# Ten more plain weight splits on VectorE, the first two weights loaded in halves, and the last quarter's first Down outputs behind the last seventh product

## The chip, the cores and the metric

One core of one Trainium2 chip runs the whole kernel. The metric is the device time of one execution in microseconds (us), the median over several runs. Engines are named as the profile names them: PE (TensorE, the matrix unit), DVE (VectorE), ACT (ScalarE), POOL (GpSimd), SP (SyncE, which issues most loads).

## The reference, cut to what matters

A decoder of two layers over 512 tokens of width 1024, all in float32. Each layer is a half-step feed-forward block, a token mixer of three head groups, a second half-step feed-forward block and a norm:

```python
for l in range(2):
    h = x + 0.5 * swiglu(rms_norm(x, ffn1_norm[l]), ffn1_w1[l], ffn1_w3[l], ffn1_w2[l])
    n = rms_norm(h, mix_norm[l])
    u_conv, q, k, v, q_mem = jnp.split(n @ w_in[l], splits, axis=-1)
    y_conv = conv_module(u_conv, ...)       # GLU, causal depthwise conv of 31 taps over 384 channels, LayerNorm, swish
    y_swa = sliding_window_attention(q, k, v, swa_sinks[l])   # after QK-norm and rotary
    y_mem = memory_attention(qm, mk, mv)
    h = h + jnp.concatenate([y_conv, y_swa, y_mem], axis=-1) @ w_out[l]
    h = h + 0.5 * swiglu(rms_norm(h, ffn2_norm[l]), ffn2_w1[l], ffn2_w3[l], ffn2_w2[l])
    x = rms_norm(h, final_norm[l])

def swiglu(x, w1, w3, w2):                   # w1, w3: 1024 x 2816, w2: 2816 x 1024
    return (jax.nn.silu(x @ w1) * (x @ w3)) @ w2
```

## The kernel before, in words

The residual stream `h` stays on chip as 128 partitions x 8 blocks x 512 tokens. Weights come from HBM in units of 128 x 1024 (512 KB) or less into a `raw` buffer, of which there are three.

**Split products.** PE multiplies rounded operands, so every operand is kept as a high part and a low part, and one product term is three matmuls (`mm3`): high x high (L161), low activation x high weight (L162), high activation x low weight (L163). A plain projection (`project`) has 8 such terms, 24 matmuls of 128 x 512. What makes the parts of a weight is `weights(src, cols, on)`:
- with `on` = V it calls `split`: ACT copies `raw` to `whi` (L135), VectorE subtracts to get `wlo` (L136);
- with `on` = G it calls `split_by_dma`: ACT copies `raw` to `whi` (L140) and its negative to `wlo` (L141), and then POOL issues a DMA that loads the same weights from HBM a second time and adds them onto `wlo` (L142).

There are four `whi`/`wlo` pairs, so a pair comes free when the product before the last three has been multiplied. The same line L136 also makes the low parts of activations (`xlo`, `ml`, `glo`).

**A feed-forward block.** 22 hidden blocks of 128. The first four (`PLAIN`) are computed plainly, eight projections (`up`): w1 and w3 of each. Then nine pairs of hidden blocks follow, each by the seven products of a Strassen scheme (`up_pair`) on half-width operands: matmuls of 128 x 256 into the PSUM tiles `po` and `pt`, with the high parts of operands made by ACT and the low parts by VectorE. The Down projection (w2) runs in four `QUARTERS` of 6, 6, 6 and 4 hidden blocks. `begin(d)` loads a Down weight for output block d and multiplies all but its last two hidden blocks; the loop after it adds the last two, then VectorE adds the result into `h`. In the first three quarters the next pair of hidden blocks is computed first and one output is begun at a time; in the last quarter (`ahead` is 0) the first three outputs are begun ahead of the last seventh product's results.

**Start.** `h`, the first two weights and small tables are loaded by SP. For each of the eight blocks of `h`, ACT and VectorE make `xhi` (L145) and `xlo` (L146), and POOL squares the block (L215); VectorE adds the squares into `st` (L229). PE sums `st` over the partitions (`cf`, L186) between the second and the third projection, VectorE makes the mean (`ms`, L192), POOL takes the power -1/2 (`rsq`, L178), PE spreads it over the tokens (`pt`, L199), ACT copies it (`R`, L204), and VectorE makes the normed activations for the seven products (`n`, L256). The rotary tables (L459 to L492 on VectorE, `sn` L496 and `cs` L497 on ACT) are made in the same stretch.

**Mixer.** The convolution's 384 channels are three chunks `c` of 128; each needs two projections (GLU value and gate). They and the query projections run while VectorE does the 93 taps of the depthwise convolution, of which the 90 accumulating ones are L744. `head_scale` and its ACT squares (`hsq`, L512) stand between, with VectorE rows L514, L515 and L519.

**Order.** Every engine works through a fixed queue. A scheduler sets the order of independent instructions by its own estimate of times when the program is built; `queued()` overrides it for a block of code: the block's PE instructions are put on PE's queue right behind the last PE instruction traced before.

Of the kernel before, what the change touches and what calls it, by code (L numbers as in the profile page):

```python
# [10 lines left out]
F32 = mybir.dt.float32  # L11
# [7 lines left out]
P = 128  # L19
D = 1024  # L20
# [19 lines left out]
UNIT = 1024  # L40
# [19 lines left out]
def trunk(ctx: ExitStack, tc: tile.TileContext, xT, memT, pos, w1a, w3a, w2a, w1b, w3b, w2b,  # L60
          wconv, wqk, wvm, wmem, wout, gains, small, rows, consts, out):
    nc = tc.nc
    V, G, A, T = nc.vector, nc.gpsimd, nc.scalar, nc.tensor
# [3 lines left out]
    wst = ctx.enter_context(tc.tile_pool(name="wst", bufs=4))  # L67
# [8 lines left out]
    def queued():  # L76

        return tc.issue_after(tail[0].ins)
# [18 lines left out]
    def raw_tile(src, cols):  # L97
        raw = wst.tile([P, UNIT], F32, tag="raw", name="raw", bufs=3)
        nc.sync.dma_start(raw[:, 0:cols], src)
        return raw  # L100
# [3 lines left out]
    gn = const.tile([P, L, 5, KD], F32, name="gn")  # L104
    nc.sync.dma_start(gn, gains)
    first = []
    for k in range(KD):
        nc.sync.dma_start(h[:, k, :], xT[:, k, :])
        if k in (0, 3):
            first.append(raw_tile((w1a, w3a)[k // 3][0, 0], D))  # L110
    cst = const.tile([P, P + 256 + 32], F32, name="cst")
    nc.sync.dma_start(cst, consts)
    ident = cst[:, 0:P]
# [20 lines left out]
    def split(hi, lo, x, on):  # L134
        A.activation(hi, x, AF.Copy)  # L135
        on.tensor_tensor(out=lo, in0=x, in1=hi.bitcast(F32), op=ALU.subtract)  # L136
# [11 lines left out]
    def pair():  # L148
        return (wst.tile([P, UNIT], F32R, tag="whi", name="whi"), wst.tile([P, UNIT], F32R, tag="wlo", name="wlo"))

    def weights(src, cols, on):
        raw = first.pop(0) if first else raw_tile(src, cols)
        hi, lo = pair()
        if on is G:
            split_by_dma(hi[:, 0:cols], lo[:, 0:cols], raw[:, 0:cols], src)
        else:
            split(hi[:, 0:cols], lo[:, 0:cols], raw[:, 0:cols], on)
        return hi, lo
# [12 lines left out]
    def project(ps, w, x):  # L171

        for k in range(KD):
            mm3(ps, at(w, ALL, blk(k)), at(x, ALL, k, ALL), k == 0, k == KD - 1)
# [208 lines left out]
    def ffn(l, w13, w2, x, sums, factors, last, at_product, aside=None):  # L383
# [2 lines left out]

        def up(f, i):
            ps = bank([P, S], "po" if 2 * f + i in (3, 4) else "mm")
            project(ps, weights(w13[i][l, f], 1024, V if f == 0 else G), x)
            return ps  # L390

        def gate(pp, R, u, g, hi, lo):
# [29 lines left out]
        for q, (f0, nf) in enumerate(QUARTERS):  # L422
            ahead = 2 if q + 1 < len(QUARTERS) else 0
            for f in range(f0, f0 + nf + ahead, 2):
                if f not in g:
                    g[f], g[f + 1] = up_pair(l, w13, f, M)
            begun = []

            def begin(d):

                w = weights(w2[l, d, :, f0 * P : (f0 + nf) * P], nf * P, V)
                ps = bank([P, S], "mm")
                for j in range(nf - 2):
                    mm3(ps, at(w, ALL, blk(j)), g[f0 + j], j == 0, False)
                begun.append((ps, w))

            for d in range(KD):
                while len(begun) < (d + 1 if ahead or d else 3):
                    begin(len(begun))
                ps, w = begun[d]  # L440
                for j in range(nf - 2, nf):
                    mm3(ps, at(w, ALL, blk(j)), g[f0 + j], False, j == nf - 1)
                V.scalar_tensor_tensor(out=h[:, d, :], in0=ps, scalar=0.5, in1=h[:, d, :], op0=ALU.mult, op1=ALU.add)  # L443
                if not ahead:
                    last(d)
            if aside and not q:
                aside()
# [139 lines left out]
    def mixer(l, x, st, last):  # L587
# [31 lines left out]
        def conv_in(c):  # L619
            nonlocal R  # L620
            pp = []
            for i in range(2):
                with queued() if 2 * c + i < 3 else nullcontext():
                    ps = mm()
                    project(ps, weights(wconv[l, c, i], 1024, G if c == 2 else V), x)
                    pp.append(ps)
                if c == 0:
                    with queued():
                        if i == 0:
                            V.tensor_copy(rc, rms_cols(st, D))  # L630
                        else:
                            R = kept(spread(rc), "R")
            u, s = ypad[:, c, PAD:], ring("cv")
            V.tensor_tensor(out=u, in0=pp[0], in1=R, op=ALU.mult)
            V.tensor_tensor(out=s, in0=pp[1], in1=R, op=ALU.mult)
            A.activation(s, s, AF.Sigmoid)
            V.tensor_tensor(out=u, in0=u, in1=s, op=ALU.mult)
# [128 lines left out]
        for step in ORDER.split():  # L766
            f = {"c": conv_in, "q": queries, "v": values, "w": window, "r": recall, "t": taps, "s": swish}[step[0]]
# [4 lines left out]
        for d in range(KD):  # L772
            w = weights(wout[l, d, :, CCH:], 640, V)
            ps = bank([P, S], ("mm", "mm", "mm", "cf", "po", "po", "pt", "pt")[d])
# [3 lines left out]
        for d in range(KD):  # L778
            w = weights(wout[l, d, :, 0:CCH], CCH, V)
# [3 lines left out]
            last(d)  # L783


    st = Stat("st", on=G)
    nxt = Next(gn[:, 0, N_FFN1], (st, None))
    for d in range(KD):
        nxt(d)

    def stages(st, gain):
# [5 lines left out]
    for l in range(L):  # L797
        x, new = nxt.x, Stat("st")
# [110 lines left out]
```

## Time and profile before

| | |
|---|---|
| time, median of 3 runs | 1847.12 us (1841.6, 1847.12, 1849.46) |
| profiled execution | 1840.85 us, its span 1839.1 us |
| granted clock, mean | 0.988 |
| PE busy | 1777.9 us (97% of the span) |
| DVE busy | 1297.8 us (71%) |
| ACT busy | 895.5 us (49%) |
| POOL busy | 188.3 us (10%) |
| DMA | 248.87 MB, of which 56.63 MB in the queue of POOL's transfers |

The profile is of one execution. A row of the timeline gives an instruction's start, its duration, its engine, line and tiles, and in brackets how long the engine sat idle ahead of it and what ended that wait. Matmuls are pipelined: a row of 0.39 us for 128 x 512 is followed by the next one 0.23 us later at full clock and 0.43 us later at half clock, so the distance of starts is what a matmul costs. VectorE's rows overlap by some 0.07 us in the same way.

### The profile page before, as it was taken

Reading aid. Unit: us, or ns where it says so; the run is one execution under the profiler, and the core shown is the slowest. Engines: PE = TensorE matmul, PEld = TensorE weight load, DVE = VectorE, ACT = ScalarE, POOL = GpSimd, SP = SyncE. Lnnn points to the kernel's source line nnn. Section 1 sums busy time; section 2 is a strip of 40 time slices with the busy share of each in tenths; the row PEclk is TensorE's granted clock in tenths of the full one; section 3 lists DMA queues with packets and bytes.
Section 4 is the critical chain, followed back from the end, with each engine's and each line's share of the span. In section 5 each row is a group of like instructions: output and inputs, shape, how many; then the busy total and the mean of one; then the engine's idle time right before and its main releaser. Section 6 shows DMA issues by size and latency. Waiting matters only on the chain.

```text
span 1839.1 us, 28085 instructions
## 1 busy us (share of the span) xinstructions
PE 1777.9 (97%) x10892; PEld 1581.9 (86%) x10892; DVE 1297.8 (71%) x1978; ACT 895.5 (49%) x1459; POOL 188.3 (10%) x194
## 2 busy tenths in 40 slices
PE   6999999998899999999999999999989999999997
PEld 5989999877677989898888898988776889898986
DVE  7967666579956866666678586666789577675755
ACT  5556444354656535453565463535456455353532
POOL 4001000005101000000010010000240010000000
PEclk8999999999999999999999999999999999999998
DMA  9565645263038556565465565643530576474622
GB/s 278 125 172 159 177 130 155 63 159 101 15 77 200 118 141 167 143 169 141 133 154 139 160 170 141 170 118 92 117 105 1 144 162 158 134 181 122 171 78 75
DMA packets 92437, 248.87 MB, mean 135 GB/s; under 512 B 9488, under 2 KB 11792, under 8 KB 92304
## 3 DMA queue, kind: packets, MB, share of 16 engines
q1 hardware_dynamic: 76752, 190.45, 34.0%
q0 software_dynamic: 15552, 56.63, 17.3%
q8 instruction: 85, 1.39, 0.3%
q14 instruction: 48, 0.39, 0.1%
HBM read 244.95 MB, written 2.10 MB: 134 GB/s over the span
## 4 chain that ended last, share of the span: by engine, by line
PE 76%; DVE 10%; issue 7%; DMA 4%; ACT 2%; POOL 1%; SPq 0%; POOLq 0%; DVEq 0%; ACTq 0%
PE mm L162 11%; PE mm L163 10%; PE mm L161 10%; PE po L163 8%; PE po L161 8%; PE po L162 8%; PE pt L161 5%; PE pt L162 5%; PE pt L163 5%; DVE there L744 3%; DVE wlo L136 1%; DMA wlo<-in_w1a 1%; DVE xlo L146 1%; DMA wlo<-in_wconv 1%; DVE st L229 1%
## 5 line engine op out<-in xcount | busy, mean ns | idle before, releaser
L135 ACT ACTIVATE whi<-raw 128x1024 fp32r<-128x1024 f32 (+4 forms) x372 | 342.3, 924 | 513.3 <-PE mm L162 263.9
L136 DVE TENSOR_TENSOR wlo<-raw,whi 128x1024 fp32r<-128x1024 f32 (+4 forms) x372 | 392.0, 1056 | 123.8 <-ACT whi L135 122.5
L162 PE MATMUL mm<-glo,whi 128*128 128x512 f32 x752 | 293.9, 391 | 1.0 <-DVE glo L136 1.0
L161 PE MATMUL mm<-ghi,whi 128*128 128x512 f32 x752 | 289.8, 391 | 5.2 <-ACT ghi L379 4.5
L163 PE MATMUL mm<-ghi,wlo 128*128 128x512 f32 x752 | 292.8, 389 | 0.0
L163 PE MATMUL po<-mh,wlo 128*128 128x256 f32 x864 | 244.6, 283 | 1.4 <-DVE wlo L136 1.4
L161 PE MATMUL po<-mh,whi 128*128 128x256 f32 x864 | 244.8, 283 | 0.0
L162 PE MATMUL po<-ml,whi 128*128 128x256 f32 x864 | 244.6, 283 | 0.0
L161 PE MATMUL pt<-xhi,whi 128*128 128x256 f32 x864 | 243.4, 283 | 1.0 <-DVE g L347 0.7
L163 PE MATMUL pt<-xhi,wlo 128*128 128x256 f32 x864 | 243.9, 283 | 0.0
L162 PE MATMUL pt<-xlo,whi 128*128 128x256 f32 x864 | 243.8, 283 | 0.0
L443 DVE SCALAR_TENSOR_TENSOR h<-mm,h 128x512 f32<-128x512 f32 x128 | 87.7, 688 | 134.5 <-PE mm L163 134.5
L161 PEld LDWEIGHTS mm<-ghi,whi 128*128 128x128 f32 x752 | 140.9, 188 | 35.9 <-ACT ghi L379 6.2
L161 PEld LDWEIGHTS pt<-xhi,whi 128*128 128x128 f32 x864 | 165.1, 192 | 3.0 <-DVE g L347 1.1
L163 PEld LDWEIGHTS po<-mh,wlo 128*128 128x128 f32 x864 | 165.8, 192 | 1.6 <-DVE wlo L136 1.6
L162 PEld LDWEIGHTS mm<-glo,whi 128*128 128x128 f32 x752 | 141.4, 188 | 30.0 <-DVE glo L136 1.9
L162 PEld LDWEIGHTS pt<-xlo,whi 128*128 128x128 f32 x864 | 165.7, 192 | 1.1
L161 PEld LDWEIGHTS po<-mh,whi 128*128 128x128 f32 x864 | 165.8, 192 | 0.9 <-ACT part L366 0.2
L163 PEld LDWEIGHTS mm<-ghi,wlo 128*128 128x128 f32 x752 | 141.2, 188 | 29.2
L162 PEld LDWEIGHTS po<-ml,whi 128*128 128x128 f32 x864 | 165.8, 192 | 0.6
L163 PEld LDWEIGHTS pt<-xhi,wlo 128*128 128x128 f32 x864 | 165.5, 192 | 0.0
L744 DVE SCALAR_TENSOR_TENSOR there<-ypad,par,there 128x512 f32<-128x512 f32 x180 | 133.7, 759 | 0.7
(272 smaller groups left out, 3306.4 us busy)
## 6 DMA issues: line engine op xcount, KB each, us to landing
raw<-in_w2a SPq DMA_DIRECT2D x48, 384.0 KB, 3.7
raw<-in_w2b SPq DMA_DIRECT2D x48, 384.0 KB, 4.0
raw<-in_w1a SPq DMA_DIRECT2D x26, 512.0 KB, 3.7
raw<-in_w3a SPq DMA_DIRECT2D x26, 512.0 KB, 4.3
raw<-in_w1b SPq DMA_DIRECT2D x26, 512.0 KB, 3.8
raw<-in_w3b SPq DMA_DIRECT2D x26, 512.0 KB, 3.7
wsum<-in_w1a SPq DMA_DIRECT2D x18, 512.0 KB, 4.5
wsum<-in_w3a SPq DMA_DIRECT2D x18, 512.0 KB, 4.5
```

The source lines that it names most:

```text
L135: A.activation(hi, x, AF.Copy)
L136: on.tensor_tensor(out=lo, in0=x, in1=hi.bitcast(F32), op=ALU.subtract)
L146: V.scalar_tensor_tensor(out=lo, in0=x, scalar=col, in1=hi.bitcast(F32), op0=ALU.mult, op1=ALU.subtract)
L161: T.matmul(ps, a[0], b[0], start=first, stop=False, **more)
L162: T.matmul(ps, a[0], b[1], start=False, stop=False, **more)
L163: tail[0] = T.matmul(ps, a[1], b[0], start=False, stop=last, **more)
L229: V.tensor_tensor(out=self.sums[0], in0=self.sums[0], in1=sq, op=ALU.add)
L443: V.scalar_tensor_tensor(out=h[:, d, :], in0=ps, scalar=0.5, in1=h[:, d, :], op0=ALU.mult, op1=ALU.add)
L744: V.scalar_tensor_tensor(out=cv[:, c, :], in0=ypad[:, c, j : j + S], scalar=conv_w[:, c, j : j + 1], in1=cv[:, c, :], op0=ALU.mult, op1=AL ...
```

## The change

Four edits:
1. The first two weights (w1 and w3 of hidden block 0) are loaded as halves of 128 x 512, the first of them ahead of `h`, and their parts are made half by half, on VectorE as before.
2. In layer 0's first feed-forward block the six other plain weights are split on VectorE (`split`) and not by DMA; so are the two weights of convolution chunk 2, in both layers. In total ten second loads of 512 KB, with their DMA issues on POOL and their negative copies on ACT, go, and ten subtracts of 128 x 1024 come.
3. Of the eight initial squares of `h`, two (blocks 2 and 5) are taken by ACT, six by POOL.
4. In the last quarter of each Down projection the first three `begin(d)` stand in `queued()`.

```diff
     first = []
+    for w in (w1a, w3a):
+        first.append(wst.tile([P, UNIT], F32, tag="raw", name="raw", bufs=3))
+    halves = [slice(i * 512, i * 512 + 512) for i in range(2)]
+    nc.sync.dma_start(first[0][:, halves[0]], w1a[0, 0, :, halves[0]])
     for k in range(KD):
         nc.sync.dma_start(h[:, k, :], xT[:, k, :])
-        if k in (0, 3):
-            first.append(raw_tile((w1a, w3a)[k // 3][0, 0], D))
+        if k == 1:
+            nc.sync.dma_start(first[0][:, halves[1]], w1a[0, 0, :, halves[1]])
+        if k in (4, 5):
+            nc.sync.dma_start(first[1][:, halves[k - 4]], w3a[0, 0, :, halves[k - 4]])
...
     def weights(src, cols, on):
-        raw = first.pop(0) if first else raw_tile(src, cols)
         hi, lo = pair()
+        if first:
+            raw = first.pop(0)
+            for c in halves:
+                split(hi[:, c], lo[:, c], raw[:, c], V)
+            return hi, lo
+        raw = raw_tile(src, cols)
...
-            project(ps, weights(w13[i][l, f], 1024, V if f == 0 else G), x)
+            project(ps, weights(w13[i][l, f], 1024, V if f == 0 or l == 0 and w13[0] is w1a else G), x)
...
                 while len(begun) < (d + 1 if ahead or d else 3):
-                    begin(len(begun))
+                    with nullcontext() if ahead or d else queued():
+                        begin(len(begun))
...
-                    project(ps, weights(wconv[l, c, i], 1024, G if c == 2 else V), x)
+                    project(ps, weights(wconv[l, c, i], 1024, V), x)
...
-    st = Stat("st", on=G)
+    st = Stat("st")
     nxt = Next(gn[:, 0, N_FFN1], (st, None))
     for d in range(KD):
+        st.on = G if d % 3 < 2 else None
         nxt(d)
```

The line numbers of the kernel after are higher: L161 to L163 become L172 to L174, L136 becomes L142, L146 becomes L152, L229 becomes L240, L459 to L497 become L471 to L509, L744 becomes L756.

VectorE's queue at the start, before, from the last squares to the first rows of the rotary tables (`st` is the sum of squares, `ms` the mean, `ypad` a buffer that the tables use as scratch):

```order
L146 SCALAR_TENSOR_TENSOR xlo<-h,gn,xhi 128x512 x3
L229 TENSOR_TENSOR st<-st,sq 128x512
L131 TENSOR_SCALAR nsink<-rw 128x12
L537 TENSOR_TENSOR gmem<-rw 128x64
L229 TENSOR_TENSOR st<-st,sq 128x512 x3
L192 TENSOR_SCALAR ms_230<-cf 128x4
L466 CAST pf<-posi 128x4
L467 TENSOR_TENSOR ypad<-cst,pf 128x128
L459 TENSOR_SCALAR ypad<-ypad 128x128
```

The same place after:

```order
L152 SCALAR_TENSOR_TENSOR xlo<-h,gn,xhi 128x512 x2
L137 TENSOR_SCALAR nsink<-rw 128x12
L549 TENSOR_TENSOR gmem<-rw 128x64
L240 TENSOR_TENSOR st<-st,sq 128x512 x2
L142 TENSOR_TENSOR wlo<-raw,whi 128x1024
L240 TENSOR_TENSOR st<-st,sq 128x512
L142 TENSOR_TENSOR wlo<-raw,whi 128x1024
L203 TENSOR_SCALAR ms_236<-cf 128x4
L478 CAST pf<-posi 128x4
L479 TENSOR_TENSOR ypad<-cst,pf 128x128
```

The subtract of the third plain weight now stands ahead of the last sum of squares, that of the fourth ahead of `ms`. Two more stand among the first rows of the tables, the last two among the gates of the plain blocks; 28 rows of the tables and the six products `sg`, `cg` with them, which all stood ahead of `n` (L256), now stand behind it.

PE's queue at the end of the last seven-product pair of a block, before (`pt` is the last seventh product, `mm` with `ghi`, `glo` are Down outputs; the row with x3 is the first that needs the gated result of this pair):

```order
L162 MATMUL pt<-xlo,whi 128x256
L163 MATMUL pt<-xhi,wlo 128x256
L161 MATMUL mm<-ghi,whi 128x512
L162 MATMUL mm<-glo,whi 128x512
L163 MATMUL mm<-ghi,wlo 128x512
L161 MATMUL mm<-ghi,whi 128x512
L162 MATMUL mm<-glo,whi 128x512
L163 MATMUL mm<-ghi,wlo 128x512
L161 MATMUL mm<-ghi,whi 128x512 x3
```

The same place after:

```order
L174 MATMUL pt<-xhi,wlo 128x256
L172 MATMUL mm<-ghi,whi 128x512
L173 MATMUL mm<-glo,whi 128x512
L174 MATMUL mm<-ghi,wlo 128x512
L172 MATMUL mm<-ghi,whi 128x512
L173 MATMUL mm<-glo,whi 128x512
L174 MATMUL mm<-ghi,wlo 128x512
L172 MATMUL mm<-ghi,whi 128x512
L173 MATMUL mm<-glo,whi 128x512
L174 MATMUL mm<-ghi,wlo 128x512
L172 MATMUL mm<-ghi,whi 128x512
L173 MATMUL mm<-glo,whi 128x512
```

Of the 18 matmuls of the three begun outputs, six stood behind the last seventh product before; the other twelve stood between the last two products and ahead of them. All 18 stand behind it now, and the last two products follow each other at once.

VectorE's queue in layer 0's mixer, before, where the two projections of convolution chunk 2 run (`hv` is a row of `head_scale`, `cg`, `sg` are rotary factors):

```order
L744 SCALAR_TENSOR_TENSOR there<-ypad,par,there 128x512
L515 TENSOR_SCALAR hv_4113<-hs_4112 128x8
L744 SCALAR_TENSOR_TENSOR there<-ypad,par,there 128x512
L533 TENSOR_TENSOR cg<-cs,rw 128x4x64
L659 TENSOR_TENSOR gg<-gg 128x512
L533 TENSOR_TENSOR cg<-cs,rw 128x4x64
L744 SCALAR_TENSOR_TENSOR there<-ypad,par,there 128x512 x2
L136 TENSOR_TENSOR wlo<-raw,whi 128x640
```

After:

```order
L756 SCALAR_TENSOR_TENSOR there<-ypad,par,there 128x512
L527 TENSOR_SCALAR hv_4113<-hs_4112 128x8
L142 TENSOR_TENSOR wlo<-raw,whi 128x1024
L756 SCALAR_TENSOR_TENSOR there<-ypad,par,there 128x512
L142 TENSOR_TENSOR wlo<-raw,whi 128x1024
L545 TENSOR_TENSOR cg<-cs,rw 128x4x64
L671 TENSOR_TENSOR gg<-gg 128x512
L142 TENSOR_TENSOR wlo<-raw,whi 128x640
```

The two new subtracts of 128 x 1024 stand right behind `hv`, one tap apart.

## Prediction

> **What bounds the kernel now.** I read the busy times first, then PE's waits, then the timeline at each wait. The page's first line, and PE's waits, each with their total, their number and the longest:
>
> ```profile
> PE 1777.9 (97%) x10892; PEld 1581.9 (86%) x10892; DVE 1297.8 (71%) x1978; ACT 895.5 (49%) x1459; POOL 188.3 (10%) x194
> ```
>
> ```profile
> PE mm L161 <- ACT whi L135: 7.2, 1, 7.2
> PE mm L163 <- DMA wlo<-in_wconv: 5.0, 2, 2.7
> PE mm L161 <- ACT ghi L379: 4.5, 4, 1.1
> PE po L163 <- DMA wlo<-in_w1a: 2.1, 1, 2.1
> PE mm L163 <- DMA wlo<-in_w1a: 2.0, 1, 2.0
> ```
>
> PE is the bound, so only time taken out of PE's own row counts. The change touches all five of these, 20.8 us in sum, of which 7.2 is mostly the wait for the first bytes; two more places stand in the rows below. Beside the waits stands the clock. The windows below have PE busy time, granted clock, DMA share and GB/s in slices at the start (first two) and in layer 0's mixer:
>
> ```profile
> 23.89:27.31 3.42, 2.60 (x10) 0.67 0.71 111
> 30.72:34.13 3.41, 3.41 (x9) 0.50 1.04 259
> 450.56:453.97 3.41, 0.72 (x2) 0.67 0.99 224
> 453.97:457.39 3.42, 3.13 (x7) 0.50 1.02 278
> ```
>
> After a wait of about 2 us PE runs at half clock until it has been fully busy for some 3.4 us: a wait is paid a second time.
>
> The Trainium skill, "TensorE: Matmul & The Clock Gate", section "The two states you'll see" of the clock gate, drops the clock after an idle window of about 3.4 us. The trace does not agree in the letter: PE had worked 0.72 us in the slice in which the clock fell. By the page's rule no wait left over in the start below would cost clock, and the sum would be 1.7 us better; I go by the rows.
>
> **The start (edits 1 to 3).** Rows of PE, then of ACT and VectorE:
>
> ```profile
> 24.64 1.53 PE L186 MATMUL cf<-onesq,st 128*128 128x1 f32 x8 [1.79 <-DVE st L229]
> 26.04 0.77 PE L161 MATMUL mm<-xhi,whi 128*128 128x512 f32 x1
> 29.29 0.80 PE L163 MATMUL mm<-xhi,wlo 128*128 128x512 f32 x1 [2.05 <-DMA wlo<-in_w1a]
> 37.20 1.05 PE L199 MATMUL pt<-cst,rsq 128*128 128x128 f32 x8
> 46.32 0.50 PE L163 MATMUL po<-xhi,wlo 128*128 128x512 f32 x1 [2.14 <-DMA wlo<-in_w1a]
> 36.49 0.31 ACT L496 ACTIVATE sn<-ypad 128x128 f32<-128x128 f32 x1 [10.12 <-DVE ypad L492]
> 39.92 0.57 ACT L204 ACTIVATE R<-pt 128x512 f32<-128x512 f32 x1
> 40.53 2.08 DVE L256 SCALAR_TENSOR_TENSOR n<-h,gn,R 128x512 f32<-128x512 f32 x3 [0.67 <-ACT R L204]
> ```
>
> Up to 24.64 VectorE sets the pace, and its groups between 0 and 130 us cost:
>
> ```profile
> L136 DVE TENSOR_TENSOR wlo<-raw,whi 128x1024 fp32r<-128x1024 f32 x12 | 15.3, 1278 | 1.2 <-ACT whi L135 0.9
> L146 DVE SCALAR_TENSOR_TENSOR xlo<-h,gn,xhi 128x512 fp32r<-128x512 f32 x8 | 9.0, 1149 | 2.7 <-ACT xhi L145 2.7
> L380 DVE SCALAR_TENSOR_TENSOR glo<-g,ghi 128x512 fp32r<-128x512 f32 x4 | 2.6, 682 | 0.0
> ```
>
> The `xlo` rows take 1149 ns, the like rows of `glo`, made when POOL is quiet, 682 ns. One added subtract (1.14 us from start to start: 1.22 where POOL is quiet, as the like 128x1024 row of L376 further down has it, less the rows' overlap) goes ahead of the last sum of squares; against it stand two fewer POOL squares beside VectorE and first bytes that come 256 KB sooner. SP issues two more loads for the halves, POOL ten fewer accumulating ones, so POOL's powers and `wsum` loads wait for less than before; I cost both at nothing. I take the column sums at 23.5 us, 1.1 earlier (between 22.0, if every `xlo` came down to 682 ns, 8 x 0.47 = 3.7 less the 1.14, and 24.6, if nothing is won).
>
> The Trainium skill, "SBUF — State Buffer", section "Who interferes with whom", says that VectorE with two SBUF inputs and GpSimd share a port pair and lock each other out. It speaks against subtracts put on VectorE beside POOL's squares; the trace agrees (1149 against 682 ns). By it the one subtract that stands ahead of the last sum could cost 1149/682 times its 1.14, 0.8 us more, within my bounds.
>
> From there: column sums and the bank take 1.4 us (24.64 to 26.04, the third product's first start), the product's 24 matmuls at 0.227 us take 5.45, and one window at half clock costs 1.7, since PE still idles ahead of the sums. Before, this product lasted from 26.04 to 37.20, 11.2 us, with the 2.05 us wait for the accumulating DMA in it. So PE spreads at 32.0 and not at 37.20, 5.2 earlier. `R` came 2.7 us behind that only because ACT stood in its queue behind `sn`, 10.12 us on VectorE's tables; the tables are behind now, and `R` is ready 1.05 + 0.57 and some 0.2 us after the spread begins, t_R = 33.8 against 40.5 (32.1 with no half clock, 35.5 with two windows of it). The later 2.14 us wait goes too, so PE, left alone, would be 5.2 + 2.1 = 7.3 us ahead at the first seven-product pair, which follows the eighth product.
>
> What is late next is VectorE, which took over two more subtracts behind `R` and the tables that moved there:
>
> ```profile
> 46.00:92.00 46.00, 45.68 (x297) 41.99 (x298) 43.37 (x60) 23.70 (x33) 2.58 (x3) 1.00 0.51 125
> 92.00:138.00 46.00, 46.00 (x268) 40.83 (x267) 30.71 (x46) 23.38 (x39) 1.73 (x2) 1.00 0.61 172
> 40.53:105.66 65.13, 59.15 (x82) 1.00 0.57 145
> 26.22:40.53 14.31, 12.37 (x56) 0.68 1.03 232
> 104.70 0.96 DVE L136 TENSOR_TENSOR wlo<-raw,whi 128x768 fp32r<-128x768 f32 x1 [1.69 <-ACT whi L135]
> 105.63 0.40 PE L163 MATMUL mm<-ghi,wlo 128*128 128x512 f32 x1
> ```
>
> The first two rows have the busy times of PE, PEld, DVE, ACT, POOL; VectorE is 94% busy from 46 to 92 us. The next two are VectorE alone. The first of them runs from `R` to the use of the first Down weight's low part at 105.63: 59.15 busy, 0.96 of it the second Down subtract, so 58.2. To this come 2 x 1.14 = 2.3 for subtracts, and the 28 table rows and six factors, which stood in the stretch from 26.22 on: 34 of its 56 instructions, so 7.5 of its 12.37 us, where each row waits for the one before it; set among other rows they start some 0.07 us before their predecessor's end, which leaves 5.1. 65.6 of work and about 3 of waits for PE and ACT that stay, 68.6: the low part is there at 33.8 + 68.6 = 102.4, 3.2 us ahead of before. So VectorE lets the pair keep 3.2 and not 7.3. I take 3 us for the start; 0.7 if the table rows cost their 7.5, 1.5 with two windows of half clock, 7.3 if VectorE's waits shrink and PE stays the bound. Behind 105 us VectorE has room (30.71 of 46 us is its busy time from 92 to 138), so nothing further is lost.
>
> **The convolution's third chunk (edit 2), per layer.**
>
> ```profile
> 450.83 0.50 PE L161 MATMUL mm<-xhi,whi 128*128 128x512 f32 x1 [1.59 <-ACT hsq L512]
> 454.26 0.79 PE L163 MATMUL mm<-xhi,wlo 128*128 128x512 f32 x1 [2.70 <-DMA wlo<-in_wconv]
> 449.53 0.16 DVE L515 TENSOR_SCALAR hv<-hs 128x8 f32<-128x8 f32 x1
> 461.60 0.69 DVE L634 TENSOR_TENSOR ypad<-mm,R 128x512 f32<-128x512 f32 x1 [3.54 <-PE mm L163]
> 467.53 0.69 DVE L635 TENSOR_TENSOR aux<-mm,R 128x512 f32<-128x512 f32 x1 [1.41 <-PE mm L163]
> 470.00:522.00 52.00, 46.77 (x283) 34.41 (x282) 49.48 (x140) 34.67 (x123) 4.94 (x4) 0.93 0.02 7
> 1365.57 0.69 DVE L634 TENSOR_TENSOR ypad<-mm,R 128x512 f32<-128x512 f32 x1 [2.97 <-PE mm L163]
> 1371.73 0.69 DVE L635 TENSOR_TENSOR aux<-cf,R 128x512 f32<-128x512 f32 x1 [0.55 <-PE cf L163]
> ```
>
> PE loses 1.6 + 2.7 and then about 2.3 to half clock. But the mixer is VectorE's: 49.48 of 52 us busy from 470 on, and PE's loss counts only as VectorE's idle time, 3.54 + 1.41 = 4.95 us here, waiting for these projections. The new subtracts stand right behind `hv` (449.53), a tap apart, so both low parts are there by 452.6, some 1.7 us before the old one; with the half clock gone too the product ends at 461.6 - 2.7 - 2.3 = 456.6, ahead of VectorE's need even with 2 x 1.14 = 2.28 us more of rows. Net 4.95 - 2.28 = 2.7 in layer 0. In layer 1 the idle time is 2.97 + 0.55 = 3.5: net 1.2. Sum 3.9. Below: idle time unchanged and the subtracts added, -2.28 per layer, -4.6. Above: the subtracts fall into idle time that stays elsewhere, +8.5.
>
> **The last Down quarters (edit 4), four times.**
>
> ```profile
> 362.62 0.28 PE L163 MATMUL pt<-xhi,wlo 128*128 128x256 f32 x1
> 362.94 0.42 DVE L347 TENSOR_TENSOR g<-pt,part 128x256 f32<-128x256 f32 x1 [3.08 <-PE pt L163]
> 363.47 1.23 DVE L376 TENSOR_TENSOR g<-g,u 128x1024 f32<-128x1024 f32 x1
> 364.73 1.15 ACT L379 ACTIVATE ghi<-g 128x512 fp32r<-128x512 f32 x2 [1.22 <-DVE g L376]
> 365.41 0.97 PE L161 MATMUL mm<-ghi,whi 128*128 128x512 f32 x3 [1.12 <-ACT ghi L379]
> ```
>
> From the last product's start to the gated `ghi` the chain takes 365.41 - 362.62 = 2.79 us, and six matmuls (1.36 us) cover it. Eighteen last 4.08 us and cover it whole: 1.28 us per block by the distance of starts, 5.1 in all. The price could be a new wait: the last product writes the bank that VectorE's sum of the product before last reads, and the fillers between the two are gone. That sum needs about 0.32 + 0.68 + 0.1 us (start after the matmul's as in the first two rows, the 682 ns of a 128 x 512 row, and the release), the product between lasts 12 x 0.12 = 1.44 us: covered by 0.3 us. Without that cover up to 1.1 per block would go back; bounds 0.7 to 5.1.
>
> **The sum.** 3 + 3.9 + 5.1 = 12.0 us. The profiled execution took 1840.85 us, its span 1839.1 with 1.75 around it; it becomes 1828.9. It lies 6.3 below the median of the runs, 1847.12, so the forecast on that footing is 1835.
>
> **The rivals.** First: VectorE eats the first two gains. The pair at 70 to 105 us is VectorE's already, and the taps are; if the waits on it grow by 3 us at the start and the mixer's idle time moves elsewhere, only the 5.1 us stay, with perhaps 1 more: 1841. For it speaks the 94%; against it that VectorE's idle time in the mixer is named, and waits for the very products that come sooner. Second: PE stays the bound at the start. 7.3 + 3.9 + 5.1 = 16.3: 1831, and 1826 with the mixer's upper end. For it speaks that ACT and PE waits are part of VectorE's 68.6. Third, the other side: a late VectorE makes PE wait in the plain products. They last 5.45 us each and the fourth to the eighth need a subtract that stands in one queue with gates, sums and tables. If each of the six stalls by 2 us, the half clock adds 1.7 each: 6 x 3.7 = 22 us against 12.0, 1857. It decides from a stall in four of them; against it, VectorE's added rows there are 7.4 us in all, and the subtracts of the third to the sixth product stand ahead of `R`. Fourth: the change doesn't do what it says at the Down quarters, since a wait on the bank takes the place of that on `ghi`; 3 + 3.9 + 0.7 = 7.6 us are left, 1839.5.
>
> **How the numbers follow.** A measurement of this kernel can tell about 0.5%, 9.2 us, from no change. The forecast, gains of 9.3 to 16 us and its own range 1831 to 1838, gets 0.52, the PE-bound start 0.08, VectorE eating the gains 0.25, bank waits 0.07, late subtracts 0.08, of which 0.01 ends about even. So faster by over 0.5% is 0.60, within it 0.33, slower 0.07. The range takes in the second rival below and the first and the fourth above, with 2 us for the spread of the runs: 1828 to 1844.
>
> **What the profile after would show.** Start: no PE wait for an accumulating DMA of `w1a`, `cf` at about 23.5, the spread near 32, `n` near 33.8, PE waits of about 4 us in sum for `xlo` or `wlo` between 65 and 100. Mixer: no wait for `in_wconv`, full clock at 452 to 458, and VectorE's idle time ahead of the chunk's first gate row gone. Down: no wait for `ghi` at the four places. 5.2 MB fewer in POOL's queue. The forecast is wrong if VectorE's work between `R` and the first Down weight exceeds 68.6 us by as much as `R` comes early, or if the taps end no sooner.

## The result and the profile after

The kernel after takes 1832.38 us, median of 6 runs (1829.19 to 1834.45), the kernel before 1845.28 (1841.6 to 1849.46): ratio 0.9929, interval 0.9911 to 0.9947, some 13 us. The forecast was 12.0 us and 1835. The profiled execution took 1829.19 us, its span 1827.4, 11.7 less than the span before.

The page's first line and PE's waits of the kernel after, longest first, those of 1.5 us and more in total:

```profile
PE 1773.5 (97%) x10892; PEld 1579.3 (86%) x10892; DVE 1306.6 (72%) x1990; ACT 887.8 (49%) x1453; POOL 177.8 (10%) x182
```

```profile
PE pt L702 <- ACT uu L697: 9.2, 5, 4.9
PE mm L172 <- ACT xhi L151: 7.0, 3, 6.4
PE mm L745 <- ACT there L557: 4.3, 3, 2.0
PE cf L716 <- DVE glo L142: 3.4, 2, 2.2
PE mm L173 <- DVE xlo L152: 3.2, 9, 0.6
PE pt L172 <- ACT xhi L141: 2.0, 1, 2.0
PE mm L172 <- ACT hsq L524: 1.7, 3, 0.6
PE pt L173 <- DVE xlo L142: 1.5, 1, 1.5
```

No row names an accumulating DMA of `in_w1a` or `in_wconv` any more, and the four waits for `ghi` of the gate (L379 before, L390 now) are gone. New are the two waits of `pt` for `xhi` and `xlo`, 3.5 us, and the 2.2 us for `glo`. In the mixers the waits for `there` have grown from 1.3 to 4.3 us, and the longest for `uu` from 2.9 to 4.9. POOL's queue moved 51.39 MB where it was 56.63, the 5.2 MB fewer of the forecast.

Where the time went, by stages. Each number is the distance between the starts of the same two matmuls in PE's queue (numbers 0, 600, 2140 and so on of 10892), from two profiles of each kernel; the second pair comes from the experiments below:

| stage of PE's queue | before | before, 2nd | after | after, 2nd |
|---|---|---|---|---|
| first matmul starts at | 7.22 | 6.97 | 6.45 | 6.32 |
| start to the first seven-product pairs (0 to 600) | 113.58 | 115.15 | 109.66 | 110.57 |
| last Down quarter, layer 0, first block (2140 to 2240) | 16.93 | 16.93 | 15.44 | 15.44 |
| mixer, layer 0 (2330 to 3020) | 144.73 | 145.64 | 143.44 | 143.72 |
| last Down quarter, layer 0, second block (5150 to 5400) | 40.45 | 40.41 | 38.94 | 38.94 |
| last Down quarter, layer 1, first block (7440 to 7700) | 42.69 | 42.70 | 41.21 | 41.21 |
| mixer, layer 1 (7760 to 8600) | 178.06 | 182.41 | 178.11 | 180.69 |
| last Down quarter and end (10440 to 10891) | 84.78 | 84.77 | 83.31 | 84.07 |

By the first pair of profiles the start gave 3.9 + 0.8 us, the four Down quarters 5.9, the two mixers 1.2. The Down quarters repeat to 0.05 us, all but the end's second profile; the mixers of one and the same program differ by up to 4.4 us.

The start, rows of PE and then of VectorE, answering to those of before:

```profile
24.42 1.05 PE L197 MATMUL cf<-onesq,st 128*128 128x1 f32 x8 [0.70 <-DVE st L240]
25.33 0.48 PE L172 MATMUL mm<-xhi,whi 128*128 128x512 f32 x1
30.90 1.05 PE L210 MATMUL pt<-cst,rsq 128*128 128x128 f32 x8
72.67 0.39 PE L172 MATMUL pt<-xhi,whi 128*128 128x256 f32 x1 [1.98 <-ACT xhi L141]
76.17 0.38 PE L173 MATMUL pt<-xlo,whi 128*128 128x256 f32 x1 [1.53 <-DVE xlo L142]
```

```profile
21.70 2.06 DVE L142 TENSOR_TENSOR wlo<-raw,whi 128x1024 fp32r<-128x1024 f32 x1
23.68 0.68 DVE L240 TENSOR_TENSOR st<-st,sq 128x512 f32<-128x512 f32 x1
24.29 1.21 DVE L142 TENSOR_TENSOR wlo<-raw,whi 128x1024 fp32r<-128x1024 f32 x1
```

The third product starts at 25.33 and ends at 30.90 without a wait: 24 matmuls at full clock. The windows of PE say the same of the clock, 1.00 where it was 0.67 and 0.50, and the two for layer 0's mixer below them too:

```profile
23.89:27.31 3.42, 2.89 (x17) 1.00 0.86 147
30.72:34.13 3.41, 3.41 (x21) 1.00 1.07 274
443.40:446.80 3.40, 3.00 (x12) 1.00 0.15 36
446.80:450.20 3.40, 3.40 (x17) 1.00 0.68 200
```

The end of layer 0's first feed-forward block; the matmuls from 355.30 to 359.18 are the 18 of the begun outputs, the row with x3 needs `ghi`:

```profile
355.18 0.28 PE L174 MATMUL pt<-xhi,wlo 128*128 128x256 f32 x1
355.30 0.40 PE L172 MATMUL mm<-ghi,whi 128*128 128x512 f32 x1
...
359.18 0.39 PE L174 MATMUL mm<-ghi,wlo 128*128 128x512 f32 x1
359.41 0.84 PE L172 MATMUL mm<-ghi,whi 128*128 128x512 f32 x3
```

ACT has the first half of `ghi` from 357.9 on, 1.5 us ahead of PE's need (its row: `357.29 1.16 ACT L390`, two instructions).

### The profile page after: what moved, and what is told of

Same layout as the page of the kernel before. It is cut to its first block, busy times and chain, and to the rows that moved or that the text cites. A ratio compares the mean times of both kernels' runs of the same rounds, so it can differ in the third digit from the quotient of the medians.

```text
span 1827.4 us, 28061 instructions
## 1 busy us (share of the span) xinstructions
PE 1773.5 (97%) x10892; PEld 1579.3 (86%) x10892; DVE 1306.6 (72%) x1990; ACT 887.8 (49%) x1453; POOL 177.8 (10%) x182
## 3 DMA queue, kind: packets, MB, share of 16 engines
q0 software_dynamic: 14112, 51.39, 15.9%
## 4 chain that ended last, share of the span: by engine, by line
PE 77%; DVE 11%; issue 7%; DMA 2%; ACT 2%; POOL 0%; SPq 0%; DVEq 0%; POOLq 0%; ACTq 0%
PE mm L172 11%; PE mm L173 11%; PE mm L174 11%; PE po L172 8%; PE po L173 8%; PE po L174 8%; PE pt L173 5%; PE pt L172 5%; PE pt L174 5%; DVE there L756 4%; DVE wlo L142 1%; DMA wsum<-in_w3b 1%; DVE mm L731 1%; DVE xlo L152 1%; PE cf L172 1%
## 5 line engine op out<-in xcount | busy, mean ns | idle before, releaser
L141 ACT ACTIVATE whi<-raw 128x1024 fp32r<-128x1024 f32 (+4 forms) x384 | 353.1, 924 | 514.1 <-PE mm L173 248.1
L142 DVE TENSOR_TENSOR wlo<-raw,whi 128x1024 fp32r<-128x1024 f32 (+4 forms) x384 | 404.6, 1056 | 128.0 <-ACT whi L141 127.0
L174 PE MATMUL mm<-ghi,wlo 128*128 128x512 f32 x752 | 293.4, 390 | 0.0
L172 PE MATMUL mm<-ghi,whi 128*128 128x512 f32 x752 | 289.8, 392 | 0.8 <-ACT ghi L141 0.8
L174 PE MATMUL po<-mh,wlo 128*128 128x256 f32 x864 | 244.6, 283 | 1.3 <-DVE wlo L142 1.3
L172 PE MATMUL pt<-xhi,whi 128*128 128x256 f32 x864 | 243.3, 283 | 2.7 <-ACT xhi L141 2.0
L172 PE MATMUL po<-mh,whi 128*128 128x256 f32 x864 | 244.8, 283 | 0.8 <-ACT part L377 0.8
L174 PE MATMUL pt<-xhi,wlo 128*128 128x256 f32 x864 | 243.7, 283 | 0.0
L172 PEld LDWEIGHTS pt<-xhi,whi 128*128 128x128 f32 x864 | 165.1, 192 | 4.2 <-ACT xhi L141 2.4
L172 PEld LDWEIGHTS mm<-ghi,whi 128*128 128x128 f32 x752 | 141.6, 189 | 30.6 <-ACT ghi L141 1.3
L172 PEld LDWEIGHTS po<-mh,whi 128*128 128x128 f32 x864 | 165.8, 192 | 1.8 <-ACT part L377 1.2
L174 PEld LDWEIGHTS po<-mh,wlo 128*128 128x128 f32 x864 | 165.8, 192 | 1.6 <-DVE wlo L142 1.6
L174 PEld LDWEIGHTS mm<-ghi,wlo 128*128 128x128 f32 x752 | 141.6, 188 | 29.4
L174 PEld LDWEIGHTS pt<-xhi,wlo 128*128 128x128 f32 x864 | 165.5, 192 | 0.0
L756 DVE SCALAR_TENSOR_TENSOR there<-ypad,par,there 128x512 f32<-128x512 f32 x180 | 134.1, 761 | 0.7
```

The lines of the kernel that those rows point to most:

```text
L172: T.matmul(ps, a[0], b[0], start=first, stop=False, **more)
L174: tail[0] = T.matmul(ps, a[1], b[0], start=False, stop=last, **more)
L756: V.scalar_tensor_tensor(out=cv[:, c, :], in0=ypad[:, c, j : j + S], scalar=conv_w[:, c, j : j + 1], in1=cv[:, c, :], op0=ALU.mult, op1=AL ...
```

## The experiments

**The clock first: two kernels unchanged, once more.** The kernel before again, a profile alone:

> The kernel before unchanged, a second profile. In two kernels that leave the start as it was, PE took 115.1 us for its first 600 matmuls and not 113.6. Theory A (the first profile of before fell well with the clock's windows): 114.5 to 115.5 us here, and a mixer of layer 0 that is 1 to 4 us off 144.7. Rival (113.6 belongs to the program, and the two kernels' start moved for a reason of their own): 113.6 to within 0.3.

Span 1844.5 and not 1839.1. The start took 115.15 us and layer 1's mixer 182.41. Rows of the start:

```profile
24.20 1.05 PE L186 MATMUL cf<-onesq,st 128*128 128x1 f32 x8 [1.79 <-DVE st L229]
28.94 0.80 PE L163 MATMUL mm<-xhi,wlo 128*128 128x512 f32 x1 [3.10 <-DMA wlo<-in_w1a]
46.02 0.50 PE L163 MATMUL po<-xhi,wlo 128*128 128x512 f32 x1 [2.75 <-DMA wlo<-in_w1a]
```

Layer 0's mixer took 145.64, 0.9 us off and so just short of theory A's 1 to 4. Theory A holds for the start's number, but not only the clock moves: the two DMA waits were 3.10 and 2.75 us here, 2.05 and 2.14 in the first profile. So the first profile of after is 4.7 us ahead of the first profile of before at the end of this stage, and 6.0 ahead of the second.

The kernel after again, beside two of the kernels below:

> The kernel after unchanged, beside the two others on the same chip. If the granted clock's windows fall otherwise in each execution, the stages that no wait disturbs (the seven-product pairs) repeat to 0.3 us and the mixers differ by 1 to 4 us from the first profile's 143.4 and 178.1 us; if the mixers' length belongs to the program, they repeat to 0.3 us too. Time 0.993 of before; 0.4% above the kernel with the late tables.

1832.07 us, 0.9936 of before (0.9920 to 0.9952), span 1834.4. Outside the mixers, layer 0's long stretches (600 to 2140 and 3020 to 5150 in PE's queue) repeat to 0.3 us. Layer 1's do not: 5400 to 7440 took 320.52 and 322.52 us, with a slice at half clock in the second profile alone (926.03 to 929.45), and 8600 to 10440 took 275.65 and 276.46. The mixers differ by 0.3 and 2.6 us. In layer 1's mixer the mean granted clock was 0.98 in the first profile and 0.96 in the second, which is about 7 and 14 us at half clock ((1 - clock) x 2 x the stage's length). A single profile therefore says what waits, but a mixer's length only to a few us; below, sums are judged by the timed runs. The start differs too:

```profile
23.95 1.05 PE L197 MATMUL cf<-onesq,st 128*128 128x1 f32 x8 [1.08 <-DVE st L240]
24.86 0.74 PE L172 MATMUL mm<-xhi,whi 128*128 128x512 f32 x1
32.02 1.05 PE L210 MATMUL pt<-cst,rsq 128*128 128x128 f32 x8
21.50:24.91 3.41, 2.33 (x16) 1.00 0.40 68
24.91:28.33 3.42, 3.42 (x9) 0.50 0.96 235
```

The column sums came 0.5 us earlier than in the first profile, PE waited 1.08 us for them and not 0.70, and the clock fell to half behind that wait, so that the third product ended 1.1 us later than in the first profile.

**Edit 4 alone**, on the kernel before:

```diff
-                    begin(len(begun))
+                    with nullcontext() if ahead or d else queued():
+                        begin(len(begun))
```

> The kernel before with edit 4 alone. Between the two profiles PE's lead grew by 1.49, 1.51, 1.46 and 1.49 us at the four last Down quarters. Theory A (each block's 1.49 us is lasting, also where a mixer follows): span 1839.1 - 6.0 = 1833.1 us. Rival (a mixer is VectorE's, so what is won ahead of it is waited off inside it; only the two blocks without a mixer behind them count): 1839.1 - 3.0 = 1836.1 us. Second rival (the bank wait of the prediction's fourth case): a PE wait on VectorE's sum between the last two products, and a lead of 0.4 us or less per block.

1832.15 us, 0.9929 of before (0.9916 to 0.9942), 13 us; span 1830.8. The four quarters measured 15.44, 38.94, 41.21 and 83.34 us: 1.49, 1.51, 1.48 and 1.44 won, 5.9 in sum, and no new wait between the last two products. So theory A holds at the Downs; the gain of the two blocks with a mixer behind them was still there behind the mixers, so both rivals fall. That is less than half of what the runs gained. In this profile the rest lies in layer 0's mixer, 141.20 us against 144.73 and 145.64. The scheduler had ordered both mixers anew, though the edit touches no line of them, and PE's mean granted clock in layer 0's mixer was 0.98, against 0.95 in both profiles of before. How much of it is that order and how much the clock is not settled.

**Edits 1 and 3 and the six feed-forward weights**, that is the kernel after with these two lines undone:

```diff
-                    project(ps, weights(wconv[l, c, i], 1024, V), x)
+                    project(ps, weights(wconv[l, c, i], 1024, G if c == 2 else V), x)
...
-                    with nullcontext() if ahead or d else queued():
-                        begin(len(begun))
+                    begin(len(begun))
```

> The kernel before with edits 1 and 3 and the six feed-forward weights of edit 2, without the convolution's weights and without edit 4. Theory A (the start's lead is settled in the first seven-product pair by VectorE's backlog and stays from there): PE some 8.7 us ahead at the plain products, 4.7 us ahead from 100 us to the end, span 1834.4 us. Rival (the order of the mixer, which the scheduler makes from its own times, moves too and eats part): 1836 to 1837 us.

1844.07 us, 0.9985 of before (0.9974 to 0.9995), about 2.8 us; span 1837.0. PE was 9.7 us ahead of the first profile of before at the plain products and 5.3 at 97 us, a little more than theory A says. The span is the rival's: layer 1's mixer took 181.65 us, and 2.5 us of lead were left at the end. That mixer was ordered anew, but that this is the cause is not shown, since the kernel before itself took 178.06 and 182.41 there.

**Edits 1 and 3 alone**, the six weights still split by DMA:

> The kernel before with edits 1 and 3 alone: halves of the first two weights, two squares on ACT; the six weights of layer 0 still split by DMA. Theory A (the start's lead comes from the DMA waits that go with the six weights): the first product starts 0.8 us earlier, the column sums within 1 us of before, the two waits of 2.1 us for accumulating DMAs stay, span 1838 to 1839 us. Rival (the bytes of the second loads are not the limit, the first loads and the squares are): 2 us or more won by 100 us.

1841.62 us, 0.9979 (0.9966 to 0.9993); span 1838.1. PE's waits up to 60 us:

```profile
PE mm L172 <- ACT xhi L151: 6.4, 1, 6.4
PE mm L174 <- DMA wlo<-in_w1a: 3.4, 1, 3.4
PE po L174 <- DMA wlo<-in_w1a: 2.8, 1, 2.8
```

The start begins 0.8 us earlier and then takes 113.86 us, 0.5 us of lead over the first profile of before. The DMA waits stay. One part of theory A missed: the column sums came at 22.62 us, 2.0 earlier than in the first profile of before and not within 1 us of it. That lead was gone by 81 us, mainly in the two waits for the DMA, which were 2.05 and 2.14 us there. So the lead of the start comes for the most part from the six weights, as theory A says. The 3.9 us by the runs lie elsewhere again (layer 0's mixer 140.69).

**The convolution's weights alone**, on the kernel before (the first line of the diff above, the other way):

> The kernel before with the convolution's two weights per layer on VectorE alone. In the kernel after, PE's lead grew by 1.3 us in layer 0's mixer and 0.25 us in layer 1's. Theory A (this is what the edit is worth: in layer 0 VectorE's idle time of 4.95 us goes, 2.3 us of subtracts and 1.4 us of short rows that wait come; in layer 1 a lead of about 3 us at the taps' end is lost in the attention's tail): span 1839.1 - 1.6 = 1837.5 us. Rival (the tail of layer 1 was an accident of the order in the kernel after, and alone the edit is worth what was predicted): 1839.1 - 3.9 = 1835.2 us or less.

1839.93 us, 0.9975 (0.9964 to 0.9986), 4.6 us. By the runs the rival holds, with the 3.9 us of the prediction inside the interval. By the profile the mixers came to 143.88 and 176.27, 0.9 and 1.8 us less than in the first profile of before, 1.8 and 6.1 less than in the second. The span, 1838.9, is no shorter than the first one of before because the start took 115.09 us here.

**The same weights taken back to the DMA in the kernel after:**

> The kernel after with the convolution's two weights per layer split by DMA again. Theory A (the edit is worth what the profiles of before and after showed, 1.3 us in layer 0 and about nothing in layer 1): span 1828.5 to 1829.5 us. Rival (worth what was predicted, 2.7 and 1.2): 1831.3 us. Second rival (what the mixer takes is set by the order that the scheduler happens to choose, which changes with every edit): layer 0's and layer 1's mixers differ from those of the kernel after by 2 to 4 us in either direction, and the waits for the convolution's DMA come back whatever the sum does.

1831.9 us, 0.9930 (0.9912 to 0.9948): no change against 0.9929 and 0.9936 of the kernel after. The waits came back:

```profile
PE mm L174 <- DMA wlo<-in_wconv: 4.7, 2, 2.4
```

They cost nothing that these runs can tell. By the profile layer 0's mixer was 2 us longer (145.76), and layer 1's lay in between (178.81).

In layer 0's mixer the two kernels with this edit alone allow a closer look, because there PE's and VectorE's queues of this kernel are those of the kernel before, and those of the kernel above are those of the kernel after. VectorE alone in that mixer, weights by DMA (this kernel) and then weights on VectorE (the kernel above):

```profile
383.41:529.16 145.75, 118.15 (x259) 0.95 0.30 71
391.57:535.45 143.88, 121.70 (x261) 0.95 0.26 65
```

VectorE's idle time fell by 5.4 us, and its busy time rose by 3.6. Of these 3.6 the two subtracts are 2.3; the rest is rows that took longer in the new order, mainly the 90 taps (by 0.8) and four rows of 128 x 6 (by 0.7), less what overlaps. With the weights by DMA this mixer took 144.73 and 145.64 us (before), 145.76 here and 143.51 in the kernel with the start alone; with the weights on VectorE 143.44 and 143.72 (after) and 143.88. So with these orders the edit is worth some 1.2 us there, by the means, and kernels with the same order agree to some 2 us or better, which fits the second rival. In layer 1 its 2 to 4 us did not come.

**What VectorE's time in a mixer costs.** The kernel after with three of the 31 taps of each chunk left out, so that it does not compute that part of the convolution:

```diff
-            for j in range(1, TAPS):
+            for j in range(1, TAPS - 3):
```

> The kernel after with three of the 31 taps left out in each of the three chunks (that part of the convolution is not computed): 9 rows of 0.66 us, 5.9 us of VectorE, fewer per layer. Theory A (both mixers are VectorE's, so a subtract added there costs its 1.14 us): 10 to 12 us less than the kernel after. Rival (chains of short waits and half-clock windows on PE set the mixers' length, VectorE has slack): 4 us less or nothing, and then edit 2's subtracts in the mixer cost little too.

1823.77 us, 0.9890 of before (0.9872 to 0.9908), against 0.9936 of the kernel after on the same chip: 8.5 us less for 11.8 us of VectorE's rows. The mixers came to 140.37 and 173.89 us. The 8.5 us lie between theory A's 10 to 12 and the rival's 4, nearer to theory A: about 0.7 us for each us of VectorE, with a wide margin, since the intervals leave 2 to 15 us. A window in layer 0's mixer of the kernel after (busy times of PE, PEld, DVE, ACT, POOL) fits that:

```profile
430.00:512.00 82.00, 72.05 (x396) 54.93 (x395) 80.93 (x192) 48.39 (x152) 19.68 (x17) 0.96 0.12 37
```

VectorE is busy 80.93 of 82 us there. By the 0.7, an estimate, two subtracts of 1.14 us cost some 1.6 us per layer, and what they remove has to be worth more than that.

**The attention's tail in layer 1.** In the kernel after PE's lead over the kernel before (first profiles) had grown from 10.2 to 13.4 us by 1409 us and was back at 10.15 by 1422. Rows of PE, and the clock's window:

```profile
1411.74 0.39 PE L716 MATMUL cf<-cst,aux 128*128 128x128 f32 x2
1414.37 0.55 PE L716 MATMUL cf<-cst,aux 128*128 128x128 f32 x3 [2.24 <-DVE glo L142]
1412.00:1416.00 4.00, 1.39 (x8) 1.00 0.46 131
1416.00:1420.00 4.00, 4.00 (x13) 0.57 0.56 66
```

VectorE's three rows of the LayerNorm stood ahead of the attention's last rows. The edit puts them behind (`parted` holds the last two instructions of the attention's split, on ACT and VectorE):

```diff
-            f(*map(int, step[1:]))
+            if step == "s":
+                with tc.issue_after(parted[0][0].ins), tc.issue_after(parted[0][1].ins):
+                    f()
+            else:
+                f(*map(int, step[1:]))
```

> The kernel after with the LayerNorm and swish of the convolution queued on ACT and VectorE behind the last rows of attention. Theory A (in layer 1 the lead of some 3 us that the taps had at 1408 us was lost because the attention's last rows stood behind the LayerNorm's, a PE wait of 2.41 us at 1414.4 and a half-clock window behind it, 1.7 us): layer 1's mixer 3 to 4 us shorter, layer 0's within 0.5 us, span 1823.5 to 1824.5 us. Rival (the LayerNorm's results are needed as early, the out projection waits for them instead): span 1827 us or more.

1832.64 us, 0.9937 (0.9922 to 0.9953); span 1829.5, layer 1's mixer 178.94. Theory A's gain did not come. PE's waits for `glo` there are down from 3.4 to 1.2 us, one for `xlo` in that mixer is up from 0.6 to 1.9, and in the list of the whole kernel those for `pr` have grown too:

```profile
PE pt L702 <- ACT uu L697: 7.7, 5, 4.1
PE mm L172 <- ACT xhi L151: 7.4, 3, 6.5
PE mm L745 <- ACT there L557: 4.3, 3, 1.9
PE mm L173 <- DVE xlo L152: 3.7, 6, 1.9
PE pt L702 <- ACT pr L697: 2.8, 3, 1.6
```

In sum PE waits some 2 us less in layer 1's mixer than in the kernel after (11.1 us against 13.1 and 12.8), and the runs show none of it. PE's mean granted clock there was 0.96, as in the second profile of after, whose mixer took 180.69 us, and not 0.98 as in the first with 178.11. Why the runs gain nothing stays open.

**The rotary tables out of the way.** `added` holds VectorE's last Down addition of the first quarter:

```diff
-        if l == 0:
-            rope_tables()
-        tables(l)
+        with tc.issue_after(added[0].ins):
+            if l == 0:
+                rope_tables()
+            tables(l)
```

> The kernel after with the rotary tables queued on VectorE behind the Down additions of layer 0's first quarter (past 105 us, where VectorE was busy 32.1 of 46 us), and the factors made of them too. Theory A (the tables that moved behind R are what lets the start's lead shrink from 8.7 to 4.7 us): PE's waits of 2.13 and 1.69 us at 72.7 and 76.2 us go, PE is 8 to 8.7 us ahead of before at 130 us, span 1827.4 - 3.8 = 1823.6 us. Rival (the pair waits for a chain of its own operands, whatever else VectorE does): both waits stay to within 0.5 us, span 1827 us. Third: the tables meet the Down additions and PE waits there instead, 1826 to 1828 us.

1825.38 us, 0.9886 of before (0.9868 to 0.9903), span 1825.4: faster than both kernels, by the ratios 8 to 9 us faster than the kernel after. PE's first 600 matmuls took 106.75 us against 109.66 and 110.57, and PE was 7.9 us ahead of the first profile of before at their end. Layer 0's mixer, 140.74 us, is some 3 us shorter too. Of the two waits one is left, on another operand; VectorE's share between 46 and 92 us fell from 45.84 to 43.69:

```profile
46.00:92.00 46.00, 42.50 (x301) 39.84 (x300) 45.84 (x81) 25.59 (x35) 1.71 (x2) 1.00 0.40 109
92.00:138.00 46.00, 46.00 (x250) 40.02 (x249) 32.12 (x57) 21.03 (x38) 1.72 (x2) 1.00 0.59 166
```

```profile
70.99 0.39 PE L172 MATMUL po<-xhi,whi 128*128 128x256 f32 x1 [1.11 <-ACT part L372]
46.00:92.00 46.00, 44.88 (x323) 42.23 (x322) 43.69 (x59) 27.36 (x38) 2.58 (x3) 1.00 0.49 131
92.00:138.00 46.00, 46.00 (x237) 39.47 (x236) 29.32 (x52) 19.62 (x36) 0.86 (x1) 1.00 0.52 151
```

The first pair of rows is the kernel after, the other three the kernel with late tables. Theory A holds in the main: with the tables behind `R` PE lost 4.05 us of its lead between 68 and 98 us (8.74 to 4.69), without them 1.9 (9.80 to 7.93). So the tables cost about half of what was lost; the rest has another cause. The third theory falls, since PE is without a gap from 92 to 138 us in both.

**Late tables, and the convolution's weights by DMA:**

> The kernel with the late tables, and the convolution's two weights per layer split by DMA again. Two runs say opposite things of these weights: on VectorE alone against the kernel before 0.9975, [0.9964, 0.9986], taken back in the kernel after no change (0.9930 and 0.9929 of before). Theory A (VectorE's subtracts and the idle time that they remove cancel within 1 us per layer): within 2 us of the kernel with the late tables, 0.9886 of before. Rival (worth the predicted 3.9 us): 0.991 of before.

1826.28 us, 0.9905 of before (0.9887 to 0.9922), 0.9 us above the late tables by the medians, 3.5 by the ratios, whose intervals overlap. The ratio is nearer to the rival's 0.991, the medians to theory A. With the two pairs above, the convolution's part is worth 4.6, 0 and 1 to 3.5 us. Its sign is likely, its size is not settled.

## Why the prediction was right, point by point

**The sum was right, 12.0 forecast and 13 measured (9.8 to 16.4), in part by luck.** The start gave more than its term, the Down quarters a little more and the convolution less, and these misses nearly cancel. The terms cannot be checked by adding up the times of single edits: alone they gave 2.8, 4.6 and 13 us by the runs, 20 in sum, and edit 4 alone is as fast as all four (0.9929 of before, both). The stages say why. Against the kernel with edit 4 alone, the kernel after is 5 to 6 us ahead at PE's 600th matmul (116.11 and 116.89 us against 122.12). It gives back 2.2 to 2.5 us in layer 0's mixer (143.44 and 143.72 against 141.20), up to 2.7 in layer 1's, and up to 2.4 between 5400 and 7440 (320.13 there). The mixers were ordered anew in nearly every kernel, so the terms are read from the stages.

**The start**, forecast 3, is the term that was sized too low. In the four profiles with the start of before PE reaches its 600th matmul at 120.80 to 122.12 us, in the six with the start of the kernel after at 115.36 to 116.89: 5.7 us between the means, 3.9 to 6.8 between single pairs. The mechanism is as forecast: no wait for an accumulating DMA, PE ahead by 8.7 us in the first pair (forecast 7.3), and VectorE's backlog taking 4.05 us back (forecast 7.3 - 3.2 = 4.1; 3.7 to 4.4 in the six). The late tables show about half of that to be the tables' doing. What was sized too low are the two DMA waits that go: 2.05 and 2.14 us in the one profile at hand, 2.7 to 3.1 and 2.7 to 3.3 in the three others. And the window at half clock that the sum charges came in two of the six profiles alone.

Two smaller terms can be read from the six profiles with the same queues. The column sums, forecast at 23.5, came at 24.42 in the first profile and at 23.42 to 23.95 in the five others; in the first one VectorE's first sum of squares already started late, at 10.09 us and not at 9.09 to 9.62. The subtract ahead of the last sum took 2.06 or 2.07 us in all six, beside POOL's last square and the DMAs that POOL issued behind it (21.12 to 24.6 us in the first), the next one 1.21. Part of that VectorE would have waited for that square anyway: without the subtract, in the kernel with edits 1 and 3 alone, the sums came at 22.62, so it cost about the 1.14 of the forecast. The two with the window at half clock, 1.7 us in the sum, are the second profile of after, where PE spreads at 32.02 (forecast 32.0), and the kernel with the attention's rows first. PE had waited 1.06 and 1.08 us ahead of the sums in the two, 0.70 in the first profile, and 1.08 in the three others. So the length of the wait does not decide it, and what does stays open.

The prediction worked 0.8 us more for that subtract out of its rows, by what the Trainium skill, "SBUF — State Buffer", section "Who interferes with whom", says of VectorE with two SBUF inputs beside GpSimd: the trace agrees, 2.06 against 1.21. By the rule of the Trainium skill, "TensorE: Matmul & The Clock Gate", section "The two states you'll see", no wait at the start would have cost clock; in four of the six profiles none did, in two one did. In the second profile of after the clock fell at 24.91 us behind a slice in which PE had worked 2.33 of 3.41 us, and in layer 1's mixer behind one with 1.39 of 4.00 us, both without a whole idle window of 3.4 us.

**The Down quarters**, forecast 1.28 each, measured 1.44 to 1.51 in the kernel with this edit alone. The wait was sized rightly; what was left out is that PE's first matmuls behind a wait are slow. Before, the first three behind the wait took 0.80 us from 365.41 on, now they take 0.68 from 359.41 on, and the fourth, 0.26 us then, takes 0.23. That is 0.15 of the 0.2 us per block. The bank wait of the fourth rival did not come in any kernel.

**The convolution's third chunk**, forecast 3.9, is the term least borne out: 0 to 4.6 us by the runs. VectorE's idle time ahead of the chunk's two gate rows was no accident of one profile. It is there in all seven profiles with these weights by DMA, 2.3 to 3.6 and 0.6 to 1.4 us in layer 0, 2.7 to 4.0 and 0.5 to 0.6 in layer 1, and in none of the five with the weights on VectorE and all taps. The step that failed in layer 0 is the price of 2.28 us for the two subtracts: between the two orders compared above VectorE's busy time rose by 3.6 us, since other rows grew longer too, while some 5 us of idle time went, as forecast. Net that is 1.2 us by the means and not 2.7. In layer 1 the mixer's length does not settle it: 178.06 and 178.11 in the first profiles, 182.41 and 180.69 in the second, where 1.2 were forecast.

**The rivals.** First: VectorE at the start took what the forecast said and not more; in layer 0's mixer it ate about half of the gain. Second, the PE-bound start: no, but the late tables come near it (7.9 us). Third, late subtracts in the plain products: no wait there at all in the profile after. PE's waits forecast between 65 and 100 us, about 4 for `xlo` or `wlo`, were 3.5, at 72.67 for `xhi` and at 76.17 for `xlo`.

## What to carry to other kernels

A stall that is taken out of PE ahead of a stretch that another engine fills is kept only as far as that engine's queue allows: count what the change, and the scheduler, put behind it there, and move work without a due time (here the rotary tables) to where that engine has room. Matmuls that are ready anyway are worth most behind the last product whose result someone must still gate, and that gain repeats: three of the four Down quarters came out the same to 0.05 us in every kernel with this edit. In a stretch with many short waits, judge an edit by timed runs and not by two profiles, expect a scheduler to reorder places that the edit doesn't touch, and do not add up the times of single edits.

## What the runs showed of the hardware

The same program's mixer of layer 1 took 178.06 and 182.41 us in two executions (before) and 178.11 and 180.69 (after), with about 7 to 14 us of PE at half clock in it, while layer 0's long stretches outside its mixer repeat to 0.5 us. The wait for an accumulating DMA was 2.05 us in one execution and 3.10 in another at the same place. In five kernels with the same queues at the start and a wait of 1.06 to 1.08 us ahead of the column sums, the next 3.4 us ran at half clock in two executions and at full clock in three. A VectorE subtract of 128 x 1024 took 2.06 or 2.07 us while POOL squared and issued DMAs, in all six profiles with these queues, and 1.21 us right after it.
